# A two-layer attention kernel: modulation sums, rotation and group combination on VectorE instead of GpSimd

## The chip, the cores and the metric

The kernel runs on one core of a Trainium2 chip, as one program. The metric is the device time of one execution in microseconds. Before the change three executions took 1235.16 to 1239.64 us, with a median of 1238.1 us. The profile is of one further execution.

The engines have these names below: PE is TensorE (matrix products), DVE is VectorE, ACT is ScalarE, POOL is GpSimd and SP is SyncE, which here issues nearly all transfers. Each works through its own queue in order. The kernel keeps its numbers in float32 and splits each matrix operand into a high part `hi` and a low part `lo` of 32 bits each, so that one product is three matrix products: hi by hi, hi by lo, lo by hi.

## The reference

Two layers over a sequence of 512 tokens of 1024 features:

```python
def hybrid_layer(x, c, rel_table, ln_g, ln_b, w_ada, b_ada, w_in, b_gate,
                 q_norm_g, k_norm_g, w_pa, w_pb, w_o):
    mod = jax.nn.silu(c) @ w_ada + b_ada
    shift, scale, gate = jnp.split(mod, 3, axis=-1)
    u = x * (1.0 + scale[:, None, :]) + shift[:, None, :]
    proj = u @ w_in
    aq, ak, av, az, bq, bk, bv, bz, gl = jnp.split(proj, SPLIT_POINTS, axis=-1)
    y_a = mixer_a(aq, ak, av, rel_table) * jax.nn.silu(az)
    y_b = mixer_b(bq, bk, bv, q_norm_g, k_norm_g) * jax.nn.silu(bz)
    g_a, g_b = jnp.split(jax.nn.sigmoid(gl + b_gate), 2, axis=-1)
    merged = g_a * (y_a @ w_pa) + g_b * (y_b @ w_pb)
    out = merged @ w_o
    return layer_norm(DEEPNORM_ALPHA * x + gate[:, None, :] * out, ln_g, ln_b)
```

`mixer_a` is windowed attention in three groups of eight heads; the three results of a head slot are combined with weights from their softmax denominators (the group combination). `mixer_b` is attention of eight query heads on two key heads; queries and keys are normed per head and rotated (`x*cos + swapped(x)*sin`) before it. The modulation `silu(c) @ w_ada + b_ada` depends on `c` alone: 3072 numbers a layer, each a sum over 1024 rows of `w_ada`.

## The kernel before

**Weights.** Each block of 256 weight columns comes as two transfers of 512 rows into one of five buffers `raw` (class `Stream`, `RAW = 5`). `split_piece` makes from half a `raw` the high part `wh` on ACT (L173) and the low part `wl` on DVE (L174), four pieces a block. `tick` splits one piece and then calls `run_later` (work due after so many ticks) and `pump_ada`. Attention of one part and the projection chunks of the next are woven into each other by `weave` with a fixed ratio; the matrix products stand on PE in that order.

**Modulation sums.** `w_ada` is loaded in pieces of 128 x 4 x 256 into the same `raw` buffers. `ada_pool` (L289) multiplies a piece with `silu(c)` per row on POOL and adds the four quarters, three operations (L293 to L295); `ada_step` adds the second half of the rows (L313), and four ticks later `ada_sum` adds over the 128 partitions with a product against ones on PE (L90, `b<-acc,ones`), and DVE adds the bias (L325 for shift and scale, L329 for the gate). In the start-up (`start_layer0`) the shift and scale of the first layer are made in eight turns, one for each 128 features. In each turn the first half of the rows is summed on POOL (`ada0`) and the second by four multiply-adds on DVE (`ada1`, L304) into the same sum; then `modulate` makes 128 features of `u` with the sum, `low` its low part (L1049), and `products` takes them to the products for the first keys, values and queries. The later pieces, two for each of 16 sums, are summed whenever `pump_ada` finds one in a buffer.

**Rotation.** `rope_mix` norms and rotates a tile of queries or keys: a power on POOL (L514), the product with cosines on DVE (L533), the product of the swapped tile with sines on POOL (L533) and their sum on POOL (L535); DVE then multiplies with the norm (L543), which gives the tile `g` that PE transposes (L603, L621). `rope_tables` multiplies the cosines and sines with the norm weights on POOL (L493).

**Group combination.** L842 to L844, three operations of 128x512 on POOL, four times a layer. Their weights come back from a reordering in DRAM (`frow`).

**Between the layers.** `layer_norm` makes of each block of 128 tokens the normalised tile: mean and variance on DVE (L1241), a power on POOL (L1243), ACT scales and shifts (L1295). The next layer's input is `xn * (ln_g*scale) + (ln_b*scale + shift)`; the two vectors, one number per feature, are made as columns by `affine`, transposed, written to DRAM and read back as rows copied over all partitions (`affine_rows`, `arow`). POOL multiplies and adds them in row layout (L1288, L1289); `make_u` then transposes the result (L948), and ACT and DVE split it into `uh` and `ul` (L951, L952). `keep` makes the residual from the normalised tile on DVE (L1329, L1330) beside it.

## Time and profile before

| | |
|---|---|
| median of three executions | 1238.1 us (1235.16 to 1239.64) |
| profiled execution | 1239.41 us, of which the span is 1237.7 us |
| PE matrix products | 1176.5 us busy, 95% of the span |
| PE weight loads (beside the products) | 1007.4 us, 81% |
| DVE | 676.1 us, 55%, 1393 instructions |
| ACT | 519.4 us, 42%, 1092 instructions |
| POOL | 331.8 us, 27%, 286 instructions |
| transfers | 150.00 MB, 121 GB/s over the span |

The span runs from the first instruction to the last; the time of the execution has 1.7 us around it. PE's share is high, so the table by itself says little on where time can be won: one has to look for the stretches in which PE stands, and for what it waits there. DVE and POOL have time left over the whole, but not in each stage. In the chain that ended last, PE holds 76% of the span, DVE 9% and POOL 4%.

### The profile page before, as it was taken

What the parts mean: (1) busy time and instruction counts of PE and PEld (TensorE: products, weight loads), DVE (VectorE), ACT (ScalarE), POOL (GpSimd) and SP (SyncE); (2) the same over time, 40 slices, a digit from 0 to 9 for tenths busy, and PEclk for the clock granted to TensorE, in tenths of its full rate; (3) what the DMA queues carried; (4) which work ended last, traced back from release to release, by engine and by line L of the source; (5) the groups of instructions that cost most, each with busy time, mean ns of one, the idle gap of its engine ahead of it and who ended that gap; (6) DMA issues with size and microseconds to landing.
All of it is one profiled execution on the core that took longest, in us unless ns stands there. A gap on an engine that the chain in (4) does not pass through costs nothing.

```text
span 1237.7 us, 19295 instructions
## 1 busy us (share of the span) xinstructions
PE 1176.5 (95%) x7500; PEld 1007.4 (81%) x7500; DVE 676.1 (55%) x1393; ACT 519.4 (42%) x1092; POOL 331.8 (27%) x286
## 2 busy tenths in 40 slices
PE   7889799999999998999988899999999999999996
PEld 6777688888787786888988888888788778888896
DVE  7865655544445438334779654554433433844477
ACT  2345344435544554323334444444554553633220
POOL 5741654434534103000166321222200200300001
PEclk9998899999999999999999899999999999999998
DMA  9935353354445123333623242423531322333331
GB/s 279 274 112 142 118 166 107 107 154 137 129 131 149 59 82 113 96 102 121 224 91 112 77 137 73 130 84 112 171 103 53 116 68 84 123 107 98 127 112 69
DMA packets 164891, 150.00 MB, mean 121 GB/s; under 512 B 8918, under 2 KB 152142, under 8 KB 164800
## 3 DMA queue, kind: packets, MB, share of 16 engines
q1 hardware_dynamic: 162880, 143.39, 38.2%
q0 software_dynamic: 1920, 5.38, 1.3%
q8 instruction: 59, 0.97, 0.4%
q14 instruction: 32, 0.26, 0.1%
HBM read 138.54 MB, written 11.25 MB: 121 GB/s over the span
## 4 chain that ended last, share of the span: by engine, by line
PE 76%; DVE 9%; issue 4%; POOL 4%; DMA 3%; ACT 2%; SPq 1%; DVEq 0%; POOLq 0%; ACTq 0%
PE b L90 66%; PE L L90 5%; PE T L667 4%; DMA raw<-in_w_ada_dram 2%; DVE wl L174 1%; DVE acc L304 1%; POOL raw L293 1%; POOL nst L514 1%; POOL raw L294 1%; PE T L90 1%; SPq L997 0%; DVE nst L548 0%; POOL s L1288 0%; DVE g L543 0%; PE b L621 0%
## 5 line engine op out<-in xcount | busy, mean ns | idle before, releaser
L174 DVE TENSOR_TENSOR wl<-raw,wh 128x512 fp32r<-128x512 f32 x304 | 235.5, 787 | 316.3 <-ACT wh L173 315.8
L90 PE MATMUL b<-uh,wh 128*128 128x512 f32 x768 | 311.4, 406 | 3.6 <-DVE qst L624 1.7
L90 PE MATMUL b<-uh,wl 128*128 128x512 f32 x768 | 301.2, 392 | 4.5 <-DVE wl L174 4.5
L90 PE MATMUL b<-ul,wh 128*128 128x512 f32 x768 | 301.3, 392 | 0.0
L173 ACT ACTIVATE wh<-raw 128x512 fp32r<-128x512 f32 x304 | 180.0, 622 | 33.5 <-issue 24.9
L90 PEld LDWEIGHTS b<-uh,wh 128*128 128x128 f32 x768 | 145.1, 189 | 45.6 <-issue 11.5
L90 PEld LDWEIGHTS b<-uh,wl 128*128 128x128 f32 x768 | 145.1, 189 | 37.0 <-DVE wl L174 5.3
L90 PEld LDWEIGHTS b<-ul,wh 128*128 128x128 f32 x768 | 145.2, 189 | 27.3
L293 POOL TENSOR_TENSOR raw<-raw,sc 128x1024 f32<-128x1024 f32 x39 | 77.8, 1996 | 290.3 <-DMA raw<-in_w_ada_dram 235.0
L90 PE MATMUL b<-wh,uh 128*128 128x256 f32 x416 | 122.8, 295 | 0.0
L90 PE MATMUL b<-wl,uh 128*128 128x256 f32 x416 | 118.8, 286 | 0.2 <-DVE wl L174 0.2
L90 PE MATMUL b<-wh,ul 128*128 128x256 f32 x416 | 118.5, 285 | 0.0
L669 ACT ACTIVATE pt<-T 128x1024 f32<-128x1024 f32 x64 | 65.3, 1021 | 73.3 <-PE T L667 73.3
L742 ACT ACTIVATE s<-s,ast 128x256 f32<-128x256 f32 x128 | 63.5, 497 | 69.7 <-DVE ast L737 65.6
L90 PEld LDWEIGHTS b<-wh,uh 128*128 128x128 f32 x416 | 80.8, 194 | 4.8 <-issue 3.9
L90 PEld LDWEIGHTS b<-wl,uh 128*128 128x128 f32 x416 | 80.9, 195 | 0.5 <-DVE wl L174 0.4
L90 PEld LDWEIGHTS b<-wh,ul 128*128 128x128 f32 x416 | 80.4, 193 | 0.0
L90 PE MATMUL b<-g,wh 128*128 128x512 f32 x256 | 79.2, 391 | 0.0
L90 PE MATMUL b<-wh,g 128*128 128x256 f32 x384 | 71.4, 284 | 0.7 <-DVE g L1196 0.4
L90 PE MATMUL b<-pt,g 128*64 128x128 f32 x1024 | 70.0, 279 | 1.3 <-DVE gate L329 1.3
L90 PEld LDWEIGHTS b<-pt,g 128*64 128x64 f32 x1024 | 54.6, 136 | 18.9 <-issue 13.9
L667 PE MATMUL T<-idn,s 128*128 128x128 f32 x512 | 67.3, 275 | 0.5 <-DVE s L645 0.5
(180 smaller groups left out, 1849.2 us busy)
## 6 DMA issues: line engine op xcount, KB each, us to landing
raw<-in_w_in_dram SPq DMA_DIRECT2D x126, 512.0 KB
raw<-in_w_ada_dram SPq DMA_DIRECT2D x96, 256.0 KB
raw<-in_w_o_dram SPq DMA_DIRECT2D x16, 512.0 KB
g<-in_x_dram SPq DMA_DIRECT2D x16, 256.0 KB
vph<-g SPq DMA_DIRECT2D x16, 256.0 KB
g<-vph SPq DMA_DIRECT2D x16, 256.0 KB
g<-frow SPq DMA_DIRECT2D x32, 128.0 KB
raw<-in_w_pa_dram SPq DMA_DIRECT2D x8, 512.0 KB
```

Source lines behind the costliest of these rows:

```text
L90: pe.matmul(o, l, r, start=start, stop=stop, skip_group_check=True)
L173: act.activation(hi[:, d], raw[:, s], AF.Copy)
L174: dve.tensor_sub(lo[:, d], raw[:, s], hi[:, d].bitcast(F32))
L293: pool.tensor_tensor(out=raw, in0=raw, in1=sc[:, 4 * h:4 * h + 4, None].to_broadcast([128, 4, 256]), op=MUL)
L294: pool.tensor_tensor(out=raw[:, 0:2], in0=raw[:, 0:2], in1=raw[:, 2:4], op=ADD)
L304: dve.scalar_tensor_tensor(a, raw[:, k], col, a, op0=MUL, op1=ADD)
L514: pool.tensor_tensor(out=y, in0=v, in1=mhalf.to_broadcast([128, ng]), op=OP.pow)
L667: pe.transpose(t[:, 128 * j:128 * j + 128], p[:, 128 * j:128 * j + 128], idn)
L669: act.activation(pt, t, AF.Copy)
L742: act.activation(p4[:, e, b], p4[:, e, b], AF.Exp, bias=sm[:, e, b:b + 1], accum_out=s_t[:, rb, e, 1:2])
```

## The change

Four things move from POOL to DVE, and one goes. The sums of the modulation pieces are now four multiply-adds on DVE a piece (`ada_dve`), into one accumulator for both halves of the rows. A piece is summed only when it is at least `AGE = 2` ticks old. The rotation's product and sum, the tables and the group combination are DVE operations. Between the layers the affine in row layout is gone, with its way through DRAM: the transposes take the normalised tile, and ACT applies scale and shift while it copies each transposed 128x128 block out of PSUM, where a feature is a partition and the two numbers are a column of `aff`. The transposes stand one tick earlier (`LN`). In the start-up's turns the order is new: the products of a turn are split around the next turn's modulation. In the last normalisation the third block of tokens is finished on DVE like the first two.

```diff
-LN = (3, 4)
+AGE = 2
+LN = (2, 3)
...
-        a = ada_pool(raw, h)
         if h == 0:
-            accs[key] = a
-        else:
-            b = accs.pop(key)
-            pool.tensor_tensor(out=a, in0=a, in1=b, op=ADD)
-            later(4, lambda: ada_sum(l, g, [a]))
+            accs[key] = acc_tile()
+        a = accs[key]
+        for k in range(4):
+            ada_dve(a, raw, h, k, h == 0 and k == 0)
+        if h:
+            del accs[key]
+            later(2, lambda: ada_sum(l, g, a))
...
-            if key[0] == "ada":
+            if key[0] == "ada" and W.born[key, k] + AGE <= state["t"]:
...
-        for b, (to, xi, eng) in enumerate(((xq_v, xq_v, dve), (xs_v, xs_v, pool))):
-            eng.tensor_tensor(out=to.rearrange(d4, r=2, d=64), in0=xi.rearrange(d4, r=2, d=64),
+        for b, to in enumerate((xq_v, xs_v)):
+            dve.tensor_tensor(out=to.rearrange(d4, r=2, d=64), in0=to.rearrange(d4, r=2, d=64),
                               in1=gtab[a][b][:, r0:r0 + 2, None, :].to_broadcast([128, 2, nh, 64]), op=MUL)
-        pool.tensor_tensor(out=sq[:, 0:f], in0=xq_v, in1=xs_v, op=ADD)
+        dve.tensor_add(sq[:, 0:f], xq_v, xs_v)
...
-            pool.tensor_tensor(out=f12, in0=f12, in1=o12, op=MUL)
-            pool.tensor_tensor(out=f0.rearrange(ph, r=4), in0=y, in1=f0.rearrange(ph, r=4), op=MUL)
-            pool.tensor_tensor(out=y, in0=f0.rearrange(ph, r=4), in1=f12.rearrange(ph, r=4), op=ADD)
+            dve.tensor_mul(f12, f12, o12)
+            dve.tensor_mul(f0.rearrange(ph, r=4), y, f0.rearrange(ph, r=4))
+            dve.tensor_add(y, f0.rearrange(ph, r=4), f12.rearrange(ph, r=4))
...
+            pe.transpose(b[:, 128 * k:128 * k + 128], xn[:, 128 * k:128 * k + 128], idn)
+        u = G.get()
+        for k in range(4):
+            kt, ks = 4 * h + k, slice(128 * k, 128 * k + 128)
+            act.activation(u[:, ks], b[:, ks], AF.Identity, bias=aff[:, kt:kt + 1], scale=aff[:, 8 + kt:9 + kt])
...
             if more:
-                ada0(kt + 1)
+                ada(kt + 1, 0)
                 if kt < 5:
                     row_load(rows, kt + 1)
-                ada1(kt + 1, range(2))
             low(kt)
             if more:
-                ada1(kt + 1, range(2, 4))
                 load(kt + 3)
                 wsplit(kt + 1)
+                ada(kt + 1, 1)
+                products(kt, (0, 1))
                 modulate(kt + 1)
...
-            products(kt, range(4))
+            products(kt, (2, 3) if more else range(4))
...
-            elif r == 2:
-                centre()
-                for h in range(2):
-                    act.activation(xt[h], xt[h], AF.Copy, scale=y)
-                shift(0, pool)
-                later(9, lambda: shift(1, pool))
```

The orders of DVE show where the moved work stands. First one turn of the start-up, DVE, before: from one modulation (`mod`) to the next, with the low part of the weights (`wl`) and of the input (`ul`).

```order
L325 TENSOR_TENSOR mod_83<-b_297,cols 128x2
L304 SCALAR_TENSOR_TENSOR acc_342<-raw_208,sc,acc_342 128x256 x2
L1049 TENSOR_TENSOR ul<-g_303,uh 128x512
L304 SCALAR_TENSOR_TENSOR acc_342<-raw_208,sc,acc_342 128x256 x2
L1032 TENSOR_TENSOR wl_289<-s_213,wh_288 128x768
L325 TENSOR_TENSOR mod_83<-b_369,cols 128x2
```


The same turn, DVE, after:

```order
L301 TENSOR_TENSOR mod_82<-b_312,cols 128x2
L281 TENSOR_SCALAR acc_337<-raw_200,sc 128x256
L283 SCALAR_TENSOR_TENSOR acc_337<-raw_200,sc,acc_337 128x256 x3
L1020 TENSOR_TENSOR ul<-g_316,uh 128x512
L1003 TENSOR_TENSOR wl_282<-s_208,wh_281 128x768
L283 SCALAR_TENSOR_TENSOR acc_337<-raw_203,sc,acc_337 128x256 x4
L301 TENSOR_TENSOR mod_82<-b_383,cols 128x2
```


The two halves of four multiply-adds on DVE were one half of four; the first product of a sum (TENSOR_SCALAR) is new in the row, and the low part of the weights now stands ahead of the second half.

Second, DVE around the first of the later modulation pieces, before: two low halves of weights, a copy, the normed tile (L543) and the norm of the next.

```order
L174 TENSOR_TENSOR wl_1129<-raw_708,wh_1128 128x512
L174 TENSOR_TENSOR wl_1129<-raw_857,wh_1128 128x512
L659 COPY g_773<-b_1202 128x128
L543 TENSOR_TENSOR g_1212<-s_997,nst_921 128x512
L543 TENSOR_TENSOR g_1213<-s_997,nst_921 128x512
L548 TENSOR_TENSOR nst_1010<-nst_1010 128x8
```


The same place, DVE, after; `raw_1105` is the modulation piece, and what was L543 is L520.

```order
L176 TENSOR_TENSOR wl_1122<-raw_708,wh_1121 128x512
L281 TENSOR_SCALAR acc_1174<-raw_1105,sc 128x256
L283 SCALAR_TENSOR_TENSOR acc_1174<-raw_1105,sc,acc_1174 128x256 x3
L176 TENSOR_TENSOR wl_1122<-raw_857,wh_1121 128x512
L636 COPY g_773<-b_1196 128x128
L520 TENSOR_TENSOR g_1206<-s_997,nst_921 128x512
L520 TENSOR_TENSOR g_1207<-s_997,nst_921 128x512
L525 TENSOR_TENSOR nst_1010<-nst_1010 128x8
```


Between the two low halves now stand the four operations on the modulation piece; the low half of `raw_857` and all behind it come after them.

Third, DVE at the group combination in the first layer, before:

```order
L1145 TENSOR_TENSOR g_3530<-g_3530,g_4237 128x512
L174 TENSOR_TENSOR wl_4465<-raw_4297,wh_4464 128x512
L1128 TENSOR_TENSOR g_4519<-g_3342,g_4518 128x512
L174 TENSOR_TENSOR wl_4569<-raw_4334,wh_4568 128x512
L1128 TENSOR_TENSOR g_4548<-g_3530,g_4547 128x512
L174 TENSOR_TENSOR wl_4569<-raw_4334,wh_4568 128x512
```


The same place, DVE, after; the combination is L819 to L821.

```order
L1116 TENSOR_TENSOR g_3523<-g_3523,g_4237 128x512
L819 TENSOR_TENSOR g_4430<-g_4430,g_3835 128x512
L820 TENSOR_TENSOR g_4427<-g_4152,g_4427 128x512
L821 TENSOR_TENSOR g_4152<-g_4427,g_4430 128x4x128
L176 TENSOR_TENSOR wl_4465<-raw_4297,wh_4464 128x512
L1099 TENSOR_TENSOR g_4519<-g_3336,g_4518 128x512
L819 TENSOR_TENSOR g_4436<-g_4436,g_4007 128x512
L820 TENSOR_TENSOR g_4433<-g_4279,g_4433 128x512
```


Each of the two combinations puts three operations ahead of a low half.

Fourth, ACT between the layers, before: the normalised tile (L1295), and the high part of the transposed input (`uh`).

```order
L1295 ACTIVATE g_5220<-g_5220,mv_5779 128x512
L1295 ACTIVATE g_5221<-g_5221,mv_5779 128x512
L951 ACTIVATE uh<-b_5859 128x4x128
L173 ACTIVATE wh_5900<-raw_5554 128x512
L951 ACTIVATE uh<-b_5904 128x4x128
L1295 ACTIVATE g_5306<-g_5306,mv_5866 128x512
L1295 ACTIVATE g_5307<-g_5307,mv_5866 128x512
```


The same place, ACT, after:

```order
L1247 ACTIVATE g_5220<-g_5220,mv_5773 128x512
L1247 ACTIVATE g_5221<-g_5221,mv_5773 128x512
L929 ACTIVATE g_5858<-b_5853,aff 128x128 x4
L933 ACTIVATE uh<-g_5858 128x4x128
L175 ACTIVATE wh_5898<-raw_5541 128x512
L929 ACTIVATE g_5907<-b_5902,aff 128x128 x4
L933 ACTIVATE uh<-g_5907 128x4x128
L1247 ACTIVATE g_5306<-g_5306,mv_5865 128x512
L1247 ACTIVATE g_5307<-g_5307,mv_5865 128x512
```


Each `uh` now has four operations ahead of it, on blocks of 128x128.

## Rows read from the trace of the kernel before

**Rows 1.** The page, busy time, share of the span, instructions, by engine.

```profile
PE 1176.5 (95%) x7500; PEld 1007.4 (81%) x7500; DVE 676.1 (55%) x1393; ACT 519.4 (42%) x1092; POOL 331.8 (27%) x286
```


**Rows 2.** Stages, busy us (instructions) of each engine, granted clock, DMA share, GB/s.

```profile
145.00:590.00 445.00, 435.67 (x2641) 360.06 (x2640) 220.35 (x458) 200.26 (x432) 127.98 (x102) 1.00 0.40 121
610.00:690.00 80.00, 69.50 (x552) 68.02 (x551) 67.97 (x143) 27.88 (x54) 43.00 (x33) 0.96 0.37 121
```


**Rows 3.** Waits of PE, grouped: us in total, times, longest.

```profile
PE b L90 <- DVE acc L304: 7.9, 5, 2.7
PE b L603 <- DVE g L543: 5.7, 2, 4.2
PE b L90 <- POOL acc L313: 5.3, 1, 5.3
PE b L90 <- DVE wl L174: 4.7, 3, 4.2
PE b L948 <- POOL s L1289: 4.6, 4, 1.6
...
PE b L621 <- ACT g L448: 3.0, 1, 3.0
```


**Rows 4.** Groups of DVE: busy us, mean ns, idle before and its cause.

```profile
L174 DVE TENSOR_TENSOR wl<-raw,wh 128x512 fp32r<-128x512 f32 x304 | 235.5, 787 | 316.3 <-ACT wh L173 315.8
...
L304 DVE SCALAR_TENSOR_TENSOR acc<-raw,sc,acc 128x256 f32<-128x256 f32 x33 | 28.1, 852 | 2.3 <-POOL acc L295 1.1 <-DMA raw<-in_w_ada_dram 0.5
...
L533 DVE TENSOR_TENSOR g<-g,gt 128x512 f32<-128x512 f32 x8 | 5.5, 684 | 0.0
```


**Rows 5.** Timeline of DVE, start-up: start, us, instruction, idle before and its cause.

```profile
5.67 1.52 DVE L304 SCALAR_TENSOR_TENSOR acc<-raw,sc,acc 128x256 f32<-128x256 f32 x3
...
11.48 0.16 DVE L325 TENSOR_TENSOR mod<-b,cols 128x2 f32<-128x2 f32 x1 [0.24 <-PE b L90]
...
40.44 3.46 DVE L304 SCALAR_TENSOR_TENSOR acc<-raw,sc,acc 128x256 f32<-128x256 f32 x2
...
60.11 0.16 DVE L325 TENSOR_TENSOR mod<-b,cols 128x2 f32<-128x2 f32 x1 [1.03 <-PE b L90]
```


**Rows 6.** Timeline of several engines, 93 to 134 us.

```profile
93.37 1.05 ACT L448 ACTIVATE g<-b 24x512 f32<-24x512 f32 x2
...
93.89 1.26 POOL L535 TENSOR_TENSOR s<-g,s 128x512 f32<-128x512 f32 x1 [2.78 <-DVE g L533]
...
109.44 4.94 SPq L110 DMA_DIRECT2D raw<-in_w_ada_dram  x1
...
113.06 1.29 DVE L174 TENSOR_TENSOR wl<-raw,wh 128x512 fp32r<-128x512 f32 x2
...
123.32 1.89 POOL L293 TENSOR_TENSOR raw<-raw,sc 128x1024 f32<-128x1024 f32 x1 [26.41 <-DMA raw<-in_w_ada_dram]
...
133.83 1.91 PE L667 MATMUL T<-idn,s 128*128 128x128 f32 x8
```


**Rows 7.** Timeline of POOL, DVE and PE, 471 to 487 us.

```profile
471.58 1.62 POOL L842 TENSOR_TENSOR g<-g,g 128x512 f32<-128x512 f32 x1 [32.26 <-DMA g<-frow]
...
480.99 1.76 DVE L174 TENSOR_TENSOR wl<-raw,wh 128x512 fp32r<-128x512 f32 x1
...
483.39 0.63 PE L90 MATMUL b<-uh,wh 128*128 128x512 f32 x1
...
486.15 0.69 DVE L174 TENSOR_TENSOR wl<-raw,wh 128x512 fp32r<-128x512 f32 x1 [1.60 <-ACT wh L173]
```


**Rows 8.** Timeline of DVE, ACT and PE at the change of layers.

```profile
645.22 0.25 DVE L1241 BATCH_NORM_AGGREGATE mv<-bn 128x2 f32<-128x24 f32 x1
...
659.92 0.50 ACT L527 ACTIVATE s<-g 128x128 f32<-128x128 f32 x2
...
681.11 0.74 DVE L543 TENSOR_TENSOR g<-s,nst 128x256 f32<-128x256 f32 x2
...
681.57 1.66 PE L603 MATMUL b<-idn,g 128*128 128x128 f32 x6 [4.15 <-DVE g L543]
```

More of the change, by code (lines that the diff above doesn't have):

```diff
@@ L99, in __init__ @@
             self.raws = {}
+            self.born = {}
         def add(self, key, raws):
@@ L111, in prefetch @@
                 self.raws[key, k] = t
+                self.born[key, k] = state["t"]
                 self.out += 1
@@ L265, in affine @@
         dve.tensor_add(aff[:, 0:8], aff[:, 0:8], mod[l][:, 0:8])
-    arow = dsc.tile([16, 128], F32, name="arow")
-    def affine_rows(l):
-        affine(l)
-        def f():
-            b = B1.get()
-            pe.transpose(b[0:16, 0:128], aff, idn)
-            t = small.tile([16, 128], F32, tag="fr", name=fresh("fr"))
-            dve.tensor_copy(t, b[0:16, 0:128])
-            B1.put(b)
-            sp.dma_start(arow, t)
-        later(1, f)
     mod = [one.tile([128, 16], F32, name=f"mod{l}") for l in range(DEPTH)]
@@ L492, in rope_tables @@
             for b in range(2):
-                pool.tensor_tensor(out=gtab[a][b], in0=ropec[:, b],
+                dve.tensor_tensor(out=gtab[a][b], in0=ropec[:, b],
                                    in1=grow[:, a, b:b + 1].to_broadcast([128, 4, 64]), op=MUL)
@@ L1005, in load, with ada @@
             wsl[kt] = w
-        def ada0(kt):
-            if kt == 0:
-                sums[0] = [acc_tile()]
-                for k in range(4):
-                    ada_dve(sums[0][0], raws[0, 0], 0, k, k == 0)
-                del raws[0, 0]
-            else:
-                sums[kt] = [ada_pool(raws.pop((kt, 0)), 0)]
-        def ada1(kt, ks):
-            apart = kt in APART
-            if apart and 0 in ks:
-                sums[kt].append(acc_tile())
-            for k in ks:
-                ada_dve(sums[kt][-1], raws[kt, 1], 1, k, apart and k == 0)
-            if 3 in ks:
-                del raws[kt, 1]
+        def ada(kt, h):
+            if h == 0:
+                sums[kt] = acc_tile()
+            raw = raws.pop((kt, h))
+            for k in range(4):
+                ada_dve(sums[kt], raw, h, k, h == 0 and k == 0)
         def wsplit(kt):
@@ L1071, in start_layer0 @@
         warm(bk, WARM[0])
-        ada0(0)
-        ada1(0, range(4))
+        ada(0, 0)
+        ada(0, 1)
         bias_rows(rows, 0)
@@ L1258, in centre @@
                 rstd()
-            def shift(h, eng):
-                if eng is dve:
-                    dve.scalar_tensor_tensor(xt[h], xt[h], y, rows[1][h], op0=MUL, op1=ADD)
-                else:
-                    pool.tensor_tensor(out=xt[h], in0=xt[h], in1=rows[1][h], op=ADD)
-                put_out(h)
             def finish():
@@ L1269, in finish @@
                 for h in range(2):
-                    shift(h, dve)
+                    dve.scalar_tensor_tensor(xt[h], xt[h], y, rows[1][h], op0=MUL, op1=ADD)
+                    put_out(h)
             if r == 3:
@@ L1283, in layer_norm @@
             return
-        u = tmp4("s")
-        def affine_half(h):
-            uv = u[:, 512 * h:512 * h + 512]
-            pool.tensor_tensor(out=uv, in0=xt[h], in1=rows[0][h], op=MUL)
-            pool.tensor_tensor(out=uv, in0=uv, in1=rows[1][h], op=ADD)
         def normalise():
@@ L1295, in normalise @@
                 act.activation(xt[h], xt[h], AF.Identity, scale=y, bias=nb)
-        def both():
-            normalise()
-            for h in range(2):
-                affine_half(h)
-        later(1, both)
+        later(1, normalise)
         for h in range(2):
-            later(LN[h], lambda h=h: make_u(r, h, u))
+            later(LN[h], lambda h=h: make_u(r, h, xt[h]))
     def row_tiles(src, offs):
@@ L1314, in trunk_kernel @@
     nxt = None
-    late_put = []
     for l in range(DEPTH):
@@ L1320, in trunk_kernel @@
         else:
-            for t in late_put.pop():
-                G.put(*t)
             todo = deque([(r, h) for r in range(4) for h in range(2)])
@@ L1370, in trunk_kernel @@
             later(2, lambda: rope_tables(l + 1))
-            later(1, lambda: affine_rows(l + 1))
+            later(1, lambda: affine(l + 1))
         preload(4)
         if l + 1 < DEPTH:
-            rows = []
+            rows = None
             gb = row_tiles(ln_g[l], [0]) + row_tiles(ln_b[l], [0])
-            later(3, lambda: rows.extend(row_tiles(arow[:], [D, 0])))
         else:
@@ L1384, in trunk_kernel @@
                 gate_tile(l + 1, hh)
-            late_put.append(rows)
         nxt = xt
```

30 lines of the change are left out of this document (10 added, 20 removed).

## The prediction

> **What bounds the kernel now.** I read the page first. TensorE is busy 95% of the span, so all that this change can win is the 61 us in which it stands, plus what it loses at the lower clock behind a pause [rows 1]. VectorE is at 55% and GpSimd at 27%: neither bounds the whole. The table by stage then says where TensorE stands. From 145 to 590 us it is busy 435.7 of 445 us, so some 9 us lie there at most; around the change of layers (610 to 690 us) it is 69.5 of 80, and there VectorE is busy 68.0 of 80 [rows 2]. The waits of TensorE name the causes: accumulators of the modulation sums on VectorE, 7.9 us, and on GpSimd, 5.3 us; the normed and rotated tile `g` of L543, 5.7 us; a low half `wl`, 4.7 us (one of 4.2); the affine on GpSimd, 4.6 us; and `g` of L448, 3.0 us [rows 3]. All six have GpSimd in their chain or beside it, and that is what the rest of the reading is about.
>
> The groups of VectorE show the second cost. The same low half, 128x512, takes 0.69 us when GpSimd is quiet and 1.76 us beside the group combination [rows 7]; over all 304 its mean is 0.787 [rows 4]. That is 304 x 0.10 = 29 us of stretching on one line; the multiply-adds of L304 average 0.852 against 0.51 in a quiet chain [rows 4, 5], 33 x 0.34 = 11 us more. The other groups stretch too; 40 us is the lower bound of what VectorE loses beside GpSimd, and some 115 us my estimate if every group with two SBUF operands is stretched like these in the crowded stretches.
>
> **What the change costs on VectorE.** It gains 135 multiply-adds, 21 first products, and 16 rotation and table products, all 128x256, and 42 operations of 128x512 (24 of the combination, 16 of the rotation, 2 in the last normalisation). At 0.51 us (1.52 for three [rows 5]) and 0.68 us (L533 [rows 4]) this is 172 x 0.51 + 42 x 0.68 = 116 us. Its busy time would go from 676 to somewhere between 677 (all 115 us of stretching gone) and 752 (40 gone); I take 690, as GpSimd keeps only small powers and copies. GpSimd falls from 332 us to a few tens. So VectorE does the added work in about the time that it now loses. What counts is where the added work stands in its queue.
>
> A rule of the Trainium skill bears on this (SBUF — State Buffer, "SBUF: two separate sides"): a GpSimd operation and a VectorE operation with two SBUF inputs lock each other out of a shared port for the whole instruction. The rows agree in size: 1.76 us is the 0.69 us of the operation and about one more of waiting [rows 7]. By a full lock the stretching would end wholly, and the third rival below would be the forecast.
>
> **Start-up (0 to 62 us).** A turn of the eight ends with its modulation on VectorE; the first is at 11.48 and the last at 60.11, seven turns of 6.95 us. In them a pair of multiply-adds takes up to 3.46 us [rows 5]. After the change a turn holds on VectorE one first product and seven multiply-adds (8 x 0.51 = 4.1 at most), `ul` (0.69, as any quiet 128x512), `wl` (768 wide, about 1.0) and the modulation behind a sum on TensorE (estimated at 0.7): 6.5 us. Seven times 0.45 is -3 us. Bounds: 0, if the transfers, which come in at a similar pace, set the turn; -6, if TensorE's products do. I take -3.
>
> **First rotation (66 to 95 us).** GpSimd keeps the power alone; product and sum (1.26 us for a sum [rows 6]) become 0.68 each on VectorE. The chain to `g` of L448 at 93.37 [rows 6], for which TensorE waits 3.0 us [rows 3], gets 2 us shorter: -2, together -5 at this point. Bounds: 0 and -4.
>
> **First later modulation piece (105 to 150 us).** Here a wait is added. The transfer of the first later piece is issued at 109.44, because the sync queue hangs on three table writes behind L448, and it has landed at 123.32, when GpSimd starts on it [rows 6]: 29.9 us behind L448. VectorE now has its four operations in its queue between two low halves, and reaches them behind the first of the two low halves of 113.06 [rows 6]: at 113.7 on the old clock, 108.7 on the new. L448 is at 88.4 in the new kernel, so the piece lands at 118.3: VectorE stands for about 9.6 us, and behind it wait the low half of piece 857, a copy, the normed tile and the next rotation. TensorE has some 10 us of work left, then waits for the third and fourth quarter of that weight (1.2 and 4.5 us), and for the sum: by adding up the queue the sum is done at about 129, and the transposes of the next step, now at 133.8 behind the wait of 5.3 us for GpSimd's sum [rows 3, 6], come at about 132.3. Of the lead of 5 us about 2 are left: the stall costs +3. Bounds: -3, if the table writes end sooner than in the old trace, as no load stands beside them; +9, if the piece lands at the old absolute time and the step behind slips whole.
>
> **145 to 460 us.** Thirty modulation pieces, eight of them in the second layer, go from GpSimd, where they disturbed only VectorE, into VectorE's queue: 2.05 us each ahead of a low half. The half-idle VectorE of this stage (220 of 445 us [rows 2]) covers them, and the new age rule makes a piece wait for two steps before it is summed, so that its transfer has landed. The small reordering transfers on GpSimd's queue no longer stand behind its pieces, which may win a little; a burst may hit a step without slack, which may lose as much: 0. Bounds: -3 and +15 (half a microsecond on each of the thirty).
>
> **Group combination (470 to 490 us).** The six GpSimd operations from 471.58 stretch VectorE's, the low half that starts at 480.99 ends at 482.7, TensorE waits 4.2 us and then runs matmuls of 0.63 us, its lower clock [rows 3, 7]. On VectorE the combination is 2 x 3 x 0.68 = 4.1 us, split by a low half; the needed low half would be ready at 477.9, before TensorE wants it at 478.6. -4.2 and about -1.3 at the lower clock: -5.5. Bounds: -6 and 0 (if its input lands later than VectorE gets there: it landed at 471.58).
>
> **Change of layers (610 to 700 us).** GpSimd's affine, four operations of 128x512 a row block, each about as long as the 1.62 us of [rows 7], goes. In its place ScalarE does 32 pieces of 128x128 at 0.25 us (two took 0.50 [rows 8]), 8 us, of which 1.0 per transposed half stands in the chain to `ul`. The transposes can start when the normalised tile is there, two such operations earlier, but the result passes through 1 us more of ScalarE. I take half of the 4.6 us of [rows 3]: -2. On VectorE the list from L1241 at 645.22 to the end of L543 at 681.85 runs without a pause for 36.6 us [rows 8]; with quiet durations and the rotation added I sum it to 30.5. The wait of 4.2 us for L543 [rows 8] shrinks to about 1, -3, and the lower clock behind it goes, -1. Sum -6, bounds -11 and +2 (VectorE at 68.0 of 80 has no room if the stretching stays).
>
> **Behind it.** The rotations of the second layer's query blocks have the chain of the first layer's, and I give them the same: -2. Last normalisation: one row block moves to VectorE, 2 x 0.68, in part against a stretched chain: +0.2.
>
> **The sum** against the profiled run's 1239.4 us: -3 - 2 + 3 + 0 - 5.5 - 6 - 2 + 0.2 = -15.3, so 1224.1. The median of the runs shown is 1.3 us below the profiled one: 1223.
>
> **Rivals.** First, slower: VectorE's queue is in order, and each modulation piece stands ahead of a low half that TensorE needs. If the pieces land later than two steps after their issue, or a burst of 2.05 us meets a step without slack, TensorE loses on each. The point is 15.3 / 30 = 0.5 us a piece; at 0.7 us a piece and the gains kept it is 1223 + 21 = 1244, at 1 us 1253. For it: the first piece does just that. Against it: later pieces are issued with an idle sync queue, and VectorE is half idle. The Trainium skill (Perfetto Trace Analysis, "Optimizing Scalar/DVE Operations") speaks against this change where VectorE is saturated, and for leaving work on GpSimd there. In this trace that holds for the change of layers alone. 10%.
>
> Second, no change: the chains around the change of layers are as long through ScalarE (4 x 0.25 + 0.6 a half) as through GpSimd, start-up is set by its transfers, and the stall of the first piece is +6. Left are -5.5 and some -2: about 1235. For it: two of the three large terms are chains, not loads. 18%.
>
> Third, more: all stretching goes and with it all of the waits in [rows 3] but one microsecond each and the lower clock behind them, and the first piece lands early: -28, so 1210. For it: the lock-like stretching. Against it: the queue shown for the first piece. 17%.
>
> **How the numbers follow.** My forecast has 55%, 1215 to 1231 by its own bounds. About 0.5%, 6.2 us, can be told from no change here. Faster by more than that (below 1232) are the forecast and the third rival, 72%; within it the second, 18%; slower the first, 10%. The range from 1206 to 1243 leaves out the tail of the third rival and most of the first.
>
> **What would show it.** Low halves at 0.69 us nearly everywhere and a VectorE total near 690; start-up's last modulation near 57; a VectorE pause of some 10 us at 109 to 118 for a modulation load, with TensorE waiting on `wl` and the sum behind it; no TensorE wait at the combination; L603's wait near 1 us. Waits of VectorE for modulation loads in other places, or TensorE waits for `wl` in the middle of more than 10 us, would prove it wrong.

## The result, and the profile after

The changed kernel takes 1223.24 us (median of four, 1222.73 to 1224.42); the kernel before took 1236.63 us beside it (1233.64 to 1239.64). The ratio is 0.9884, with a 95% interval from 0.9861 to 0.9908: 1.2% faster. The forecast was 1223, in a range from 1206 to 1243. The sum came out; three of its terms did not, and they cancelled. The change is -13.4 us between these medians and -16.7 us between the spans of the two profiled executions; the forecast's sum was -15.3.

The page after, busy time and share by engine [rows 1]:

```profile
PE 1169.3 (96%) x7491; PEld 1000.9 (82%) x7491; DVE 682.7 (56%) x1606; ACT 529.8 (43%) x1122; POOL 51.4 (4%) x79
```

GpSimd has gone from 331.8 to 51.4 us, and VectorE, which took the work over, from 676.1 to 682.7 (690 was forecast). The groups of VectorE say why (line, operation, shapes, count, busy us, mean ns, idle before) [rows 4]:

```profile
L176 DVE TENSOR_TENSOR wl<-raw,wh 128x512 fp32r<-128x512 f32 x304 | 205.9, 688 | 300.8 <-ACT wh L175 300.3
L283 DVE SCALAR_TENSOR_TENSOR acc<-raw,sc,acc 128x256 f32<-128x256 f32 x168 | 81.4, 484 | 5.3
...
L821 DVE TENSOR_TENSOR g<-g,g 128x512 f32<-128x512 f32 x8 | 8.7, 1088 | 0.3
L820 DVE TENSOR_TENSOR g<-g,g 128x512 f32<-128x512 f32 x8 | 8.6, 1077 | 0.0
...
L819 DVE TENSOR_TENSOR g<-g,g 128x512 f32<-128x512 f32 x8 | 5.5, 684 | 0.0
```

The low half is at 688 ns over all 304, where it was at 787; the multiply-add at 484, where it was at 852. Two of the combination's three operations take 1.08 us and not 0.68; these two read or write with a stride of four elements (no run changes the stride alone).

The stages (length, then busy us of PE, PEld, DVE, ACT, POOL, granted clock, share of the transfer engines, GB/s) [rows 2]:

```profile
145.00:590.00 445.00, 444.58 (x2732) 369.94 (x2731) 239.55 (x574) 201.40 (x432) 7.41 (x18) 1.00 0.41 122
610.00:690.00 80.00, 67.79 (x525) 65.54 (x524) 59.49 (x144) 46.41 (x100) 15.44 (x15) 0.96 0.34 108
```

From 145 to 590 us TensorE now stands 0.4 us, where it stood 9.3. Around the change of layers (the window lies 15 us later in the program than it did) it is busy 67.8 of 80. Its waits [rows 3]:

```profile
PE b L90 <- DVE acc L283: 5.7, 7, 1.6
PE b L90 <- DVE wl L176: 5.5, 2, 3.5
PE b L925 <- ACT g L1247: 5.3, 4, 1.8
PE b L580 <- DVE g L520: 5.2, 2, 3.6
...
PE L L90 <- DVE qst L601: 2.5, 1, 2.5
...
PE b L90 <- ACT wh L175: 2.2, 1, 2.2
PE b L598 <- ACT g L425: 1.9, 1, 1.9
```

GpSimd releases none of them any more. The wait for the normalised tile (L925, 4.6 us on GpSimd's affine before, 5.3 us on ScalarE now) and for the rotated keys (L580, 5.7 before, 5.2 now) have hardly changed. To see where the 16.7 us of the two spans went, the starts of the 304 low halves (with the 12 operations of the same line on other tiles) were matched one by one, with modulations and exponentials between them. "Lead" is how much earlier the changed kernel is at the end of a stage:

```
stage (us, old kernel)     forecast   measured   lead so far
start-up, 0-60               -3         -4.0        4.0
first rotation, 66-108       -2         -2.3        6.3
first later piece, -157      +3         +2.2        4.1
145-460                       0         -5.1        9.2
combination, 470-490         -5.5       -5.7       14.9
change of layers, 610-723    -6         -2.0       16.9
behind it                    -2         -0.2       17.1
last normalisation           +0.2       +0.4       16.7
```

Start-up, first turn and last, on VectorE [rows 5]; the columns are start, us, instruction, and idle before with its cause:

```profile
11.59 0.16 DVE L301 TENSOR_TENSOR mod<-b,cols 128x2 f32<-128x2 f32 x1 [0.24 <-PE b L90]
...
56.08 0.16 DVE L301 TENSOR_TENSOR mod<-b,cols 128x2 f32<-128x2 f32 x1 [0.70 <-PE b L90]
```

From the second turn on a turn takes 6.13 us (6.5 forecast). At the first later piece [rows 6]:

```profile
92.15 3.07 SPq L435 DMA_DIRECT2D tz<-tvec  x1
...
103.57 4.82 SPq L111 DMA_DIRECT2D raw<-in_w_ada_dram  x1
...
116.82 0.35 DVE L281 TENSOR_SCALAR acc<-raw,sc 128x256 f32<-128x256 f32 x1 [9.36 <-DMA raw<-in_w_ada_dram]
...
119.39 0.39 PE L90 MATMUL b<-wl,uh 128*128 128x256 f32 x1 [3.55 <-DVE wl L176]
...
122.45 0.58 PE L90 MATMUL b<-wh,uh 128*128 128x256 f32 x1 [2.21 <-ACT wh L175]
```

VectorE stands 9.4 us for the load (9.6 forecast), and TensorE 3.6, 2.2 and 2.0 us behind it. At the combination TensorE does not stand at all; the low half behind it is at its quiet length [rows 7]:

```profile
466.60 1.09 DVE L820 TENSOR_TENSOR g<-g,g 128x512 f32<-128x512 f32 x1
...
468.63 0.67 DVE L176 TENSOR_TENSOR wl<-raw,wh 128x512 fp32r<-128x512 f32 x1
```

At the change of layers [rows 8]:

```profile
612.68 1.48 ACT L929 ACTIVATE g<-b,aff 128x128 f32<-128x128 f32 x4
...
632.56 0.26 DVE L1212 BATCH_NORM_AGGREGATE mv<-bn 128x2 f32<-128x24 f32 x1
...
632.86 1.48 ACT L929 ACTIVATE g<-b,aff 128x128 f32<-128x128 f32 x4
...
641.00 0.69 DVE L934 TENSOR_TENSOR ul<-g,uh 128x512 fp32r<-128x512 f32 x1 [1.36 <-ACT uh L933]
...
665.73 1.40 PE L580 MATMUL b<-idn,g 128*128 128x128 f32 x6 [3.64 <-DVE g L520]
```

Four pieces on ScalarE take 1.48 us, not 1.0; VectorE waits for the high half behind them (1.36 us here); and TensorE still waits 3.6 us for the rotated keys.

### The profile page after: what moved, and what is told of

It is laid out like the page before. It is cut to its first block, busy times and chain, and to the rows that moved or that the text cites. A ratio compares the mean times of both kernels' runs of the same rounds, so it can differ in the third digit from the quotient of the medians.

```text
span 1221.0 us, 19211 instructions
## 1 busy us (share of the span) xinstructions
PE 1169.3 (96%) x7491; PEld 1000.9 (82%) x7491; DVE 682.7 (56%) x1606; ACT 529.8 (43%) x1122; POOL 51.4 (4%) x79
## 4 chain that ended last, share of the span: by engine, by line
PE 82%; DVE 10%; ACT 3%; DMA 3%; issue 1%; SPq 1%; POOL 1%; DVEq 0%; POOLq 0%
PE b L90 71%; PE L L90 6%; PE T L644 5%; DMA raw<-in_w_ada_dram 2%; DVE acc L283 1%; DVE wl L176 1%; POOL nst L491 1%; ACT g L929 0%; SPq L979 0%; DMA s<-in_w_in_dram 0%; PE b L598 0%; DVE nst L488 0%; DVE g L1228 0%; DVE s L512 0%; DVE s L510 0%
## 5 line engine op out<-in xcount | busy, mean ns | idle before, releaser
L176 DVE TENSOR_TENSOR wl<-raw,wh 128x512 fp32r<-128x512 f32 x304 | 205.9, 688 | 300.8 <-ACT wh L175 300.3
L283 DVE SCALAR_TENSOR_TENSOR acc<-raw,sc,acc 128x256 f32<-128x256 f32 x168 | 81.4, 484 | 5.3
L90 PEld LDWEIGHTS b<-pt,g 128*64 128x64 f32 x1024 | 55.3, 138 | 17.7 <-issue 12.6
```

Source lines behind the costliest of these rows:

```text
L90: pe.matmul(o, l, r, start=start, stop=stop, skip_group_check=True)
L176: dve.tensor_sub(lo[:, d], raw[:, s], hi[:, d].bitcast(F32))
L283: dve.scalar_tensor_tensor(a, raw[:, k], col, a, op0=MUL, op1=ADD)
```

## The experiments

Each is compared with the kernel before on its own chip; there that took 1239.9 to 1240.4 us, so that the changed kernel would be at 0.9884 x 1240 = 1225.6. Finer than the medians, low halves were matched with those of the changed kernel; "at 463 to 483: +5.7" says that the distance to the changed kernel grew by 5.7 us there. Such a distance comes from one profiled execution of each kernel. Where an edit touches nothing, distances move too: between 660 and 705 us by -1.6 in `comb_pool`, +1.5 in `comb_twice` and +0.9 in `tz_pool`, with other granted clocks behind like waits. A distance of 1.5 us by itself is therefore not clear of the scatter.

**The combination back on GpSimd (`comb_pool`).**

```diff
-            dve.tensor_mul(f12, f12, o12)
+            pool.tensor_tensor(out=f12, in0=f12, in1=o12, op=MUL)
...
```

> The changed kernel with the group combination alone put back on GpSimd (six operations of 128x512 at each of the two layers' ends of attention). Theory 1 (stretching): VectorE's operations beside it go back from 0.69 to about 1.7 us, the low half at the combination of the first layer is late, TensorE waits about 4 us and loses about 1.3 at the lower clock: 5 us slower than the changed kernel (1228), all of it at one place near 465 us. Theory 2 (the gain there was only a shift caused by what comes before it in the queue): no new wait, 1223.

1229.92 us, ratio 0.9925 (0.9902 to 0.9948). At 463 to 483: +5.7, as theory 1 said. TensorE's wait is back, 4.24 us where [rows 3] has 4.2:

```profile
474.93 0.80 PE L90 MATMUL b<-uh,wl 128*128 128x512 f32 x1 [4.24 <-DVE wl L176]
```

**The combination on VectorE, and idle work beside it on GpSimd (`comb_twice`).**

```diff
+            pool.tensor_copy(scr[:, 0:1], f12[:, 0:1])
+            for _ in range(6):
+                pool.tensor_tensor(out=scr, in0=scr, in1=scr, op=MUL)
             dve.tensor_mul(f12, f12, o12)
```

> The combination stays on VectorE. In addition GpSimd does twelve multiplications of 128x256 on a tile of its own that nobody reads, released by the arrival of the combination's weights. Theory 1 (a GpSimd operation stretches VectorE's by itself, without any result being waited for): VectorE's two-input operations there take 1.3 to 1.8 us instead of 0.69, the low half is late and TensorE waits 2 to 5 us: 1226 to 1229. Theory 2 (the cost was that the combination on GpSimd is slow and is waited for): no wait, 1223.

1229.68 us, ratio 0.9921 (0.9893 to 0.9949). At 463 to 483: +4.0, and +1.5 each at the change of layers and at the second layer's combination. The rows:

```profile
464.63 3.11 POOL L823 TENSOR_TENSOR scr<-scr 128x256 f32<-128x256 f32 x3
...
465.14 1.10 DVE L176 TENSOR_TENSOR wl<-raw,wh 128x512 fp32r<-128x512 f32 x1
...
468.32 0.98 DVE L1121 TENSOR_TENSOR g<-g,g 128x512 f32<-128x512 f32 x1
...
473.69 0.80 PE L90 MATMUL b<-uh,wl 128*128 128x512 f32 x1 [2.70 <-DVE wl L176]
```

Nobody waits for what GpSimd does here (VectorE has no idle time between these operations), and still the operations of 0.69 us take 1.0 to 1.1 us while it runs, those with a stride 1.4 instead of 1.08, and TensorE waits 2.7 us. So stretching alone can cost 4.0 us at this place. That is not a part of the 5.7 us of `comb_pool`: here VectorE also has the combination in its queue, and GpSimd's load is another one. (The stretching is smaller than in [rows 7], where GpSimd's operations are 128x512 and not 128x256; that their size makes the difference was not tested.) In the Trainium skill (SBUF — State Buffer, "SBUF: two separate sides") this is an exclusive lock on a port that the two engines share, and the loser stands for the whole instruction; the rows agree that both are late, GpSimd's too: 6.17 us for six, 1.03 each, where the 16 sums of this size in the kernel before take 0.81.

**The later modulation pieces back on GpSimd (`later_pool`).**

```diff
+        a = ada_pool(raw, h)
         if h == 0:
-            accs[key] = acc_tile()
...
-            later(2, lambda: ada_sum(l, g, a))
+            later(4, lambda: ada_sum(l, g, a))
```

> The changed kernel with the later modulation pieces (all but start-up) summed on GpSimd as before, without the age rule and with the sum due four steps later. Theory 1: the waits of TensorE at 209 us (1.7) and at 384 to 387 us (2.7) of the old kernel come back, since GpSimd's products stretch the softmax scaling and hold up the small transfers on GpSimd's queue; between 115 and 135 us TensorE waits about 5 us for the sum on GpSimd instead of the 7.7 it now waits behind VectorE's stall. In all 3 to 6 us slower than the changed kernel: 1226 to 1229. Rival (the pieces cost the same wherever they stand): 1223 or, with the stall of VectorE gone, 1220.

1228.97 us, ratio 0.9919 (0.9887 to 0.995). By 153: -2.6 (VectorE no longer stands, but TensorE waits 6.55 us for the sum); at about 203: +1.7; at 358 to 390: +5.8; at the change of layers: +1.5. The wait for the sum, and the two places in the middle:

```profile
127.98 1.23 PE L90 MATMUL b<-acc,ones 128*128 128x256 f32 x2 [6.55 <-POOL acc L300]
...
200.92 1.89 POOL L280 TENSOR_TENSOR raw<-raw,sc 128x1024 f32<-128x1024 f32 x1 [5.40 <-DMA raw<-in_w_ada_dram]
...
201.89 2.61 DVE L629 TENSOR_SCALAR s<-s,bst 128x512 f32<-128x512 f32 x2
...
204.89 0.50 PE L90 MATMUL b<-uh,wh 128*128 128x512 f32 x1 [1.60 <-DVE qst L608]
...
365.45 1.63 POOL L281 TENSOR_TENSOR raw<-raw 128x512 f32<-128x512 f32 x1
...
367.84 0.80 POOL L786 DMA_DIRECT2D fscr<-st  x1
...
374.82 1.15 DVE L795 TENSOR_TENSOR ft<-st0p,st 128x16 f32<-128x16 f32 x1 [6.63 <-DMA st0p<-fscr]
...
379.53 0.28 PE L807 MATMUL b<-idn,ft 128*32 128x128 f32 x1 [2.13 <-DVE ft L803]
```

The softmax scaling of two 128x512 takes 2.61 us beside a GpSimd product (0.88 when quiet), and TensorE waits 1.6 us for what VectorE does next. And the small transfer of the softmax sums, issued by GpSimd, stands behind a modulation piece; VectorE waits 6.6 us for its way back, and TensorE 2.1 us for that and 0.5 us just after. The kernel before had waits of the same sum here (1.1 and 1.5 us), and lost 3.0 us by the matched low halves. The rest of the 5.8 is the clock: TensorE's granted clock is 0.74 from 375 to 385 us in `later_pool`, with products of 0.63 instead of 0.39 us, and stayed at 1.00 in the kernel before.

**The table writes issued by GpSimd (`tz_pool`).**

```diff
-            sp.dma_start(tz0, dram(td, 127, [[1024, 8], [-1, 128], [1, 384]]))
+            pool.dma_start(tz0, dram(td, 127, [[1024, 8], [-1, 128], [1, 384]]))
...
```

> The changed kernel with the three table writes from DRAM to DRAM (which hold the sync queue for 11 us ahead of the first later modulation piece) issued by GpSimd, whose queue is now nearly empty. Theory 1 (the stall of VectorE is the sync queue's hold): the piece's transfer is issued about 11 us earlier, has landed before VectorE's turn at about 108 us, and the waits of TensorE of 3.6, 2.2 and 2.0 us there go: about 6 us faster, 1217. Rival (the piece lands late because the table writes fill the transfer engines, whoever issues them): the stall stays within 2 us, 1222 to 1224; or the power of the next rotation waits behind the issues on GpSimd, and the time grows by some us.

1221.13 us, ratio 0.9857 (0.9827 to 0.9887). By 153: -2.2 only.

```profile
102.56 1.30 DVE L176 TENSOR_TENSOR wl<-raw,wh 128x512 fp32r<-128x512 f32 x2
...
103.28 1.00 SPq L111 DMA_DIRECT2D raw<-in_w_ada_dram  x2
...
115.93 0.35 DVE L281 TENSOR_SCALAR acc<-raw,sc 128x256 f32<-128x256 f32 x1 [6.36 <-DMA raw<-in_w_ada_dram]
```

The sync queue is free from 92 us, and the piece is issued at 103.28 all the same, when by the times the first low half of 102.56 has freed its buffer. It then takes 12.6 us to land beside the writes. In the changed kernel its two transfers were issued at 103.57 and 108.4 and VectorE started on it at 116.82; here both are issued by 103.8 and VectorE starts at 115.93, 0.9 us sooner, and still stands 6.4 us instead of 9.4. That falls on the side of the rival, though the stall shrank by 3 us and not by less than 2: the queue's hold is 2 us of the matter.

**The table writes ten ticks later (`tz_late`).**

```diff
-        later(10, tiles)
+        later(20, tiles)
```

> The changed kernel with the three table writes issued ten ticks later, behind the first modulation pieces and some weights. Theory (the first piece lands late because the table writes share the transfer engines with it, not only because they hold the sync queue): its transfer then takes about 5 us instead of 13, VectorE does not stand at 107 us, and TensorE's 7.7 us of waits there go: 6 us faster at 150 us. What is open is whether the writes cost as much where they now stand, as the next weights are then issued behind them: 1217 if not, 1223 if so. Rival (the buffer that the piece takes comes free too late, whatever the writes do): the stall stays above 5 us.

1227.33 us, ratio 0.9911 (0.988 to 0.994). By 153: -9.9; at 160 to 179: +14.3.

```profile
139.79 4.46 SPq L435 DMA_DIRECT2D tz<-tvec  x1
...
166.36 0.49 DVE L281 TENSOR_SCALAR acc<-raw,sc 128x256 f32<-128x256 f32 x1 [13.00 <-DMA raw<-in_w_ada_dram]
...
172.59 0.80 PE L90 MATMUL b<-uh,wh 128*128 128x512 f32 x1 [12.17 <-DVE qst L601]
```

The first piece is no longer waited for, as the theory said: issued at 102.32, nearly when it was before, it has landed when VectorE turns to it at 108.49. So the rival falls, as the buffer came free no earlier. But 20 us on, another modulation piece lands 13.0 us late for VectorE, and TensorE stands 12.2 us. The stall belongs to the writes, wherever they stand. The writes are here issued by the sync queue again; `tz_pool` shows that the queue is the small part of it.

**The writes cut in twelve (`tz_spread`), and pieces three ticks old (`spread_age3`).**

```diff
+            for n, (g, i) in enumerate([(g, i) for i in range(0, 8, 2) for g in range(3)]):
+                later(n, lambda g=g, i=i: one_head(g, i))
...
-AGE = 2
+AGE = 3
```

`one_head` writes two heads of one group's table, by GpSimd. The first kernel has only this, the second has both.

> The changed kernel with the three table writes cut into twelve of two heads each and issued by GpSimd, one a tick. Theory (the writes cost because they fill the transfer engines for some 20 us at once, and delay by that whatever weight or modulation piece is loaded beside them; whole, they cost about 8 us at 116 us and 14 at 160 when issued later): spread over some 40 us they leave each load in between late by a few us at most, VectorE stands under 4 us for the first piece, and TensorE's 7.7 us of waits between 115 and 125 us shrink to 3 or less: 4 to 7 us faster than the changed kernel. Rival (their number of small rows costs the same sum however they are spread, only in other waits): within 2 us of it.

1220.03 us, ratio 0.9841 (0.981 to 0.9872). By 119: -7.5, as the theory said (VectorE stands 1.7 us for the first piece); at 153 to 179: +4.2, where a later piece is late instead. At the end 2.1 us are left by the matched low halves, near the rival's 2, and some 5 us by the ratios of the medians, whose intervals overlap; which is nearer stays open.

> The spread table writes, and a modulation piece must now be three ticks old before its sum, which puts VectorE's first four operations behind the next low half. Theory (what is left of the spread writes' cost, TensorE's waits of 0.8, 1.6, 1.5 and 2.3 us between 117 and 157 us, comes from VectorE reaching a modulation piece before its transfer has landed): these waits shrink, 2 to 3 us faster than the spread writes alone. Rival (the buffers held longer delay the weights): the same or slower, with TensorE waiting on high or low halves elsewhere.

1215.9 us, ratio 0.9797 (0.9779 to 0.9815). By 143: -9.7; at the end -6.6, which is 4.5 more than with the spread writes alone, so the theory holds and gives more than its 2 to 3. TensorE's one wait between 95 and 180 us:

```profile
133.65 0.71 PE L90 MATMUL b<-acc,ones 128*128 128x256 f32 x2 [3.10 <-DVE qst L607]
```

Of the 7.7 us behind the first piece one wait of 3.1 us is left, and it comes from VectorE's queue: VectorE now stands at most 2.2 us for a load. This is the fastest of all: its interval lies below the changed kernel's.

**The affine between the layers back on GpSimd (`affine_pool`)**, with its rows from DRAM and `LN = (3, 4)`.

```diff
+            pool.tensor_tensor(out=uv, in0=xt[h], in1=rows[0][h], op=MUL)
+            pool.tensor_tensor(out=uv, in0=uv, in1=rows[1][h], op=ADD)
...
-            act.activation(u[:, ks], b[:, ks], AF.Identity, bias=aff[:, kt:kt + 1], scale=aff[:, 8 + kt:9 + kt])
```

> The changed kernel with the affine between the layers as before: row vectors by way of DRAM, product and sum on GpSimd ahead of the transposes, these one tick later. The rest of the change stays. Theory of the prediction (GpSimd's affine and its stretching of VectorE are what the change of layers loses): TensorE's waits there grow by 4 to 6 us, 5 us slower than the changed kernel. Theory from the trace after (the new way through ScalarE has given nearly all of that back: four pieces of 0.37 instead of 0.25 us and a high half ahead of each low half): 1 to 2 us slower, with VectorE's operations again at 1.2 to 1.8 us between 630 and 650.

1225.25 us, ratio 0.9895 (0.9859 to 0.9931). At 609 to 675: +1.5, and nothing elsewhere. VectorE's operations are stretched again, as both theories said:

```profile
631.83 1.67 DVE L1299 TENSOR_TENSOR g<-g,g 128x512 f32<-128x512 f32 x1
```

But the 4 to 6 us of the prediction's theory do not come back: it falls here. The 1.5 us are what the second theory said, and no more than the scatter.

**One activation in place of four (`one_act`).**

```diff
-        for k in range(4):
-            kt, ks = 4 * h + k, slice(128 * k, 128 * k + 128)
-            act.activation(u[:, ks], b[:, ks], AF.Identity, bias=aff[:, kt:kt + 1], scale=aff[:, 8 + kt:9 + kt])
+        act.activation(u, b, AF.Identity, bias=aff[:, 4 * h:4 * h + 1], scale=aff[:, 8 + 4 * h:9 + 4 * h])
```

> The changed kernel with one activation over 512 columns in place of the four over 128 in each half between the layers; all four blocks get the first block's scale and shift, so the numbers of the second layer are not the reference's. It takes 0.6 instead of 1.5 us, 16 halves times 0.9 = 7 us less on ScalarE there. Theory (ScalarE's pieces stand in the chain and cost the change of layers about 4 us of what was forecast): 2 to 4 us faster than the changed kernel. Rival (VectorE's list from the last block's statistics to the rotated keys sets the end; ScalarE has room): under 1 us.

1220.36 us, ratio 0.9857 (0.982 to 0.9893). At 609 to 706: -3.0, within the theory's 2 to 4. (There are 8 halves and not 16; 8 times 0.9 is the 7 us.) The waits that shrink:

```profile
PE b L580 <- DVE g L520: 4.5, 2, 2.9
PE b L925 <- ACT g L1245: 3.9, 4, 1.2
```

The row of four pieces in place of one operation costs 3 us.

**The normalisation ahead of the split (`norm_first`).**

```diff
-        later(1, normalise)
+        later_q.insert(0, [state["t"] + 1, normalise])
```

> The changed kernel with one order changed: where the normalisation of a row block and the split of the second half of the block before it fall due together, the normalisation goes first (VectorE's four small operations and ScalarE's two stand ahead of four pieces, a high half and a low half). Theory (TensorE's waits of 1.7, 1.8 and 1.2 us for the normalised tile come from the small operations standing behind a low half that itself waits for ScalarE): each shrinks by about 1 us and the chain of the last block starts earlier: 2 to 4 us faster than the changed kernel. Rival (ScalarE's row of 1.5 + 0.6 us a half is what sets the pace there): nothing is won, since the same work only changes places.

1226.09 us, ratio 0.9899 (0.9855 to 0.9942). At 609 to 643: +2.9. The theory falls: the normalised tile is waited for less (4.0 instead of 5.3 us), but the split comes later, VectorE stands for it with the next operations behind it, and TensorE waits longer for the rotated keys:

```profile
622.07 0.69 DVE L934 TENSOR_TENSOR ul<-g,uh 128x512 fp32r<-128x512 f32 x1 [3.64 <-ACT uh L933]
...
631.37 0.69 DVE L934 TENSOR_TENSOR ul<-g,uh 128x512 fp32r<-128x512 f32 x1 [3.64 <-ACT uh L933]
...
668.73 1.66 PE L580 MATMUL b<-idn,g 128*128 128x128 f32 x6 [5.24 <-DVE g L520]
```

VectorE waits 3.64 us twice, where the longest such wait was 2.54, and TensorE 5.24 us where it was 3.64. TensorE's granted clock between 600 and 680 us is 0.94 as a mean and 0.98 in the changed kernel.

**Half of the pieces on VectorE (`half_dve`).**

```diff
+            if k % 2:
+                dve.tensor_scalar(u[:, ks], b[:, ks], aff[:, 8 + kt:9 + kt], aff[:, kt:kt + 1], op0=MUL, op1=ADD)
```

> The changed kernel with two of the four pieces of 128x128 of each half between the layers on VectorE (product and sum with two columns, from PSUM) instead of ScalarE. ScalarE's part of a half falls from 1.5 to 0.75 us; VectorE gets 32 pieces of about 0.28 us. Theory (the pieces in a row on ScalarE make VectorE wait there, 8.5 us in all for the high half): 1 to 2 us faster, half of what one activation in place of four gave. Rival (VectorE's list to the rotated keys is the bound, and grows by 0.56 us a half): 1 to 4 us slower.

1234.0 us, ratio 0.9946 (0.9926 to 0.9967). At 609 to 675: +12 (some 8 us by the ratios of the medians). Neither theory has this size. The groups of the two engines, and the wait of TensorE for the normalised tile:

```profile
L930 DVE TENSOR_SCALAR g<-b,aff 128x128 f32<-128x128 f32 x16 | 6.5, 408 | 5.5 <-ACT g L932 5.5
```

```profile
L932 ACT ACTIVATE g<-b,aff 128x128 f32<-128x128 f32 x16 | 7.3, 455 | 9.9 <-DVE g L930 8.5 <-PE b L925 1.3
```

```profile
PE b L925 <- ACT g L1250: 10.5, 4, 3.6
```

A piece takes 0.41 us on VectorE (there are 16 of them, not the 32 of the expectation), and the two engines wait for each other in turn (5.5 and 8.5 us), as pieces of one tile go to and fro. TensorE's wait for the normalised tile doubles from 5.3 to 10.5 us, and its granted clock between 600 and 680 us falls from 0.98 to 0.87 as a mean. Pieces in two blocks were not tried.

**The rotation's sine product and sum back on GpSimd (`rope_pool`).**

```diff
-            dve.tensor_tensor(out=to.rearrange(d4, r=2, d=64), in0=to.rearrange(d4, r=2, d=64),
+            eng.tensor_tensor(out=to.rearrange(d4, r=2, d=64), in0=to.rearrange(d4, r=2, d=64),
...
-        dve.tensor_add(sq[:, 0:f], xq_v, xs_v)
+        pool.tensor_tensor(out=sq[:, 0:f], in0=xq_v, in1=xs_v, op=ADD)
```

> The changed kernel with the rotation's sine product and sum back on GpSimd (the tables stay on VectorE). Theory of the prediction: 2 us slower up to 95 us, where the chain to the table writes is longer again, and some 2 to 4 us more at the change of layers, where VectorE's list to the rotated keys then waits for GpSimd and is stretched by it, with TensorE's wait of 3.6 us there growing to about 5: 1227 to 1229. Rival (VectorE's list is the bound at the change of layers, and it gets shorter by eight operations there): 2 us slower at 95 us, and nothing or a gain at 665 us.

1224.53 us, ratio 0.9868 (0.9853 to 0.9884). By 119: +0.8; at 643 to 736: +1.4, no more than the scatter; the medians show no difference from the changed kernel. Both are less than expected, and the waits grow in the expected places, that for the keys from 3.6 to 4.0 us:

```profile
PE b L580 <- DVE g L520: 5.6, 2, 4.0
...
PE b L598 <- ACT g L425: 3.0, 1, 3.0
```

The wait before the table writes is 3.0 us again, as in [rows 3], and 1.9 in the changed kernel.

## Why the prediction was right, and where it was not

**What it rested on held.** The added work on VectorE cost its busy time next to nothing (6.6 us for 116 added), since the stretching beside GpSimd went; `comb_twice` shows this stretching where nothing waits for GpSimd. The combination came out at 5.7 for 5.5. `comb_pool` gives the 5.7 us back with the wait of [rows 3], and `comb_twice` shows that stretching alone can cost 4.0 us there; how the 5.7 divide between wait and clock was not taken apart.

**Start-up and first rotation** were near (-4.0 for -3, -2.3 for -2). Undoing the rotation's product and sum gives back only 0.8 of the 2.3 us; the tables, which stayed on VectorE in that experiment, or the start-up's order may hold the rest. No run undid the start-up's part, so what its 4.0 us come from, the order or the sums on VectorE, stays open.

**The first later piece** was right in time and place (a stand of 9.4 us for 9.6), and its cause was only half right. "The sync queue hangs on three table writes" is 2 us of it (`tz_pool`); the rest is that the piece is loaded while the writes are under way (12.6 us to land). `tz_late` shows it by moving the stall along with the writes, and there the buffer, freed just as late, costs nothing. How the writes hold the piece back is not shown: the 16 transfer engines were 0.55 and 0.67 busy from 95 to 105 and from 105 to 115 us in the changed kernel, and 0.86 and 0.72 in `tz_pool`, which is not full.

**145 to 460 us: the step that said 0 was -5.1,** outside of its own bounds of -3 and +15. It set a win from GpSimd's transfers against a loss from VectorE's bursts. The bursts cost nothing: the list of TensorE's waits has none between 145 and 460 us. And the losses of the kernel before in this stage come back with the pieces on GpSimd: `later_pool` loses 1.7 us at 203 us, where the kernel before lost 1.8, and 5.8 us at 358 to 390 us, where it lost 3.0 by waits of the same sum at the higher clock. The first is a stretching that the prediction left out, as it counted operations with two SBUF operands alone; the softmax scaling reads one tile and a column, and was stretched threefold. With [rows 2] at hand the step could have been bounded by the 9 us of idle time less the 4.2 of the combination: the 5 us that are left were the term's most, and it came to all of them.

**Change of layers: the step that said -6 was -2.0, and -0.2 behind it for -2.** Three things failed. The piece on ScalarE was priced at 0.25 us from a row that reads SBUF and has no bias column; in the chain it takes 0.37, and `one_act` measures that row of pieces, against one operation, at 3.0 us. The Trainium skill (ScalarE: Activation LUTs, "What ACT_TABLE_LOAD costs") has a price for a piece with two columns from which I estimate 0.39 us; the trace's 1.48 for four bears it out, and the prediction should have used it beside the row. Second, VectorE's list from the last block's statistics to the rotated keys took 33.5 us and not 30.5: its operations were as quiet as forecast, but it now stands 2.9 us for ScalarE (1.36 of them in the row above). Of these it stood 0.8 before as well; the prediction read that list as one without a pause. Third, a chain shortened on one engine was answered on the next: by the matched clock TensorE's four transposes start 2 to 3 us sooner than before, and it waited as long for them (5.3 us for 4.6). So `affine_pool` loses at most 1.5 us by going back. The wait for the rotated keys, which the prediction named as a sign (near 1 us), is 3.6 us. The second rival named this mechanism and gave it 18%; for this stage it was the right one.

**The rivals.** The first (VectorE's queue in order, a modulation piece ahead of each low half) was seen at the first piece alone, and in `tz_late` at another: it takes a load that is late by some other cause. The sentence of the Trainium skill that the prediction drew on for a saturated VectorE (Perfetto Trace Analysis, "Optimizing Scalar/DVE Operations") is followed there by a second one: VectorE and GpSimd share a port, and moving work between them might not help. The runs agree with the second: where VectorE was busiest, `affine_pool` and `rope_pool` put work back on GpSimd and won nothing (+1.5 and +1.4 us, the size of the scatter). That the total came so near to 1223 is luck in part: +4.0 at the change of layers and +1.8 behind it cancelled with -5.1 in the middle and -2.1 in the small terms, and the kernel before took 1236.6 us beside it and not the 1238.1 that the forecast started from. The range would have held it either way.

## What to carry to other kernels

In this kernel an operation on GpSimd was paid for twice: in its own time, and in that of VectorE's operations from SBUF beside it (0.69 us became 1.0 to 2.1), waited for or not. Bound a stage by the idle time of the engine that sets its end, and ask of each wait in it whether the engine to be relieved stands in its chain; what looks like noise may be the term. Large writes can delay what is loaded beside them: moving these writes moved the stall, and cutting them in pieces, with the consumers a step later, took most of it away (1215.9 us in `spread_age3`).

## What the runs showed that was not expected

The combination's operations with a stride of four elements take 1.08 us on VectorE, the one without it 0.68 (same 128x512). The softmax scaling, with one tile and a column as operands, was stretched threefold by GpSimd (0.88 to 2.61 us for two). Two of four small pieces moved from ScalarE to VectorE in turns cost 12 us, far more than their durations. Two kernels with the same 2.6 us of waits lost 3.0 and 5.8 us, as the granted clock stayed at 1.00 behind the two shorter waits (1.1 and 1.5 us) and fell behind the longer one (2.1 us).
